# Residual rows of the attention layer: stored as centred and scaled rows, finished later by GpSimd

## The chip, the cores and the metric

One Trainium2 chip, of which the kernel uses one core. TensorE (PE in the profile, PEld for its weight loads) multiplies, VectorE (DVE), ScalarE (ACT) and GpSimd (POOL) do the elementwise work, and DMAs are issued from the queues of SyncE (SP), ACT and POOL. The metric is the device time of one execution in microseconds (us).

## What is computed

A trunk of two layers on 1024 tokens of width 1024, all in float32. Layer 0 (even) mixes with a pooling mixer and a state-space scan, layer 1 (odd) with two kinds of attention, eight heads each. Each mixer and each SwiGLU is followed by a residual sum and a layer norm.

```python
def layer_norm(x, g, b):
    mu = jnp.mean(xf, axis=-1, keepdims=True)
    var = jnp.mean(jnp.square(xf - mu), axis=-1, keepdims=True)
    return ((xf - mu) * lax.rsqrt(var + LN_EPS) * g + b).astype(x.dtype)
...
    for l in range(DEPTH):
        i = l // 2
        if l % 2 == 0:
            h = even_mixer(x, ...)
        else:
            h = odd_mixer(x, ...)
        x = layer_norm(DEEPNORM_ALPHA * x + h, ln_mix_g[l], ln_mix_b[l])
        x = layer_norm(DEEPNORM_ALPHA * x + swiglu(x, ffn_w_gate[l], ffn_w_up[l], ffn_w_down[l]),
                       ln_ffn_g[l], ln_ffn_b[l])
```

The change touches the last norm of layer 0: its output x goes into layer 1 twice, transposed as the operand of the input projection, and by rows as the residual `DEEPNORM_ALPHA * x` of the odd layer.

## The kernel before

The program is written as Python generators in the order in which they are pulled; a scheduling layer then turns that order into one instruction stream for each engine, reorders a little where operands are not ready, and hands out the buffers. Nearly all tiles in SBUF come from one pool of 50 slots of 128x1024 floats (`self.slot`); a slot is given again when all who read it are done, and an instruction that writes a new tile waits for them.

A product in float32 is made of three products of split operands: a high part (a CAST on ACT, L196) and a low part, the rest (a subtraction, L204, on DVE or POOL). Operands are called `wh`, `wl` (weights), `xT` (tokens), `kh`, `kl`, `qs` (keys and queries).

`finish` (L391) ends each mixer and each SwiGLU. For each of the eight row tiles `accs[t]` (128 tokens, 128x1024, called `accr` in the trace of layer 0's SwiGLU) it takes mean and variance, and `center` (L382) makes `(x - mean) * r` in place on ACT (L385). After every fourth tile PE transposes the tiles by columns (L312) and ACT or DVE apply scale and shift of the norm on the transposed copy (L317, L319), since there they are one number for each partition; that gives `xT`. The rows themselves still lack scale and shift. Where `rows` is given (the two mixers), the centred rows are stored to memory as they are (L425), and the SwiGLU that follows finishes them one by one on POOL (`residual`, L623 to L627: load, multiply, add, store). Where it is not given (layer 0's SwiGLU before the odd layer), a generator `late` (L436) does it: two DVE operations on each row tile with the broadcast vectors `lnv` (L439, L440), and a store from SP (L442).

The odd layer, `odd`, interleaves two generators through `weave` (L45): `filler`, which yields pieces of dense PE work (projections, called units: `q0`, `k0`, `misc`, `V0`, `v0`, `q1`, ...; at the end `G0` to `G7`, which load the residual rows from `store`, L1504), and `chain`, the sequential part, which yields how many pieces of filler to pull at each point, or the name of a unit to wait for. Before the change `chain` begins with `late`, with three pieces after each row, then waits for `misc`, pulls 5 more, and runs `f_chain`: the forget gates, their logarithm (L782 to L793), cumulative sums (L821) and, in `pairs`, their broadcast to all partitions (`bias_row`, L1684). `misc` makes the forget gate's logits and the shared rotary key in two halves of 16 products (L1263); each half is read out of PSUM by ACT (L1267, L1268) and DVE (L1269, L1270). Then come eight pairs of heads, eight steps each: scores (L1594), a softmax (L1615 or L1619, L1617, L1625), transposes of the probabilities (L1646) and the product with the values (L1664).

Of the kernel before, what the change touches and what calls it, by code (L numbers as in the profile page):

```python
# [16 lines left out]
ALU = mybir.AluOpType  # L17
# [3 lines left out]
P = 128  # L21
# [60 lines left out]
class Trunk:  # L82
# [308 lines left out]
    def finish(self, accs, gb, evac, ln=None, store=None, nxt=None, rows=None):  # L391
# [3 lines left out]
        nc = self.nc  # L395
        if ln is None:
            gb = self.ln_vecs(*gb)
            for t in range(NT):
                acc = accs[t]
                mv, r = self.ln_stats(acc, evac(t))  # L400
# [17 lines left out]
        for t in range(NT):  # L418
            acc = accs[t]
            mv, r = self.ln_stats(acc, evac(t))  # L420
            if t in (0, 2):
                next(nxt)
            self.center(acc, mv, r)
            if rows is not None:
                nc.sync.dma_start(out=rows[t * P:(t + 1) * P, :], in_=acc)  # L425
            if t == 7:
                next(nxt)
            if t % 4 == 3:
                made = self.make_xT(accs, t // 4, xT, ln) if rows is None else self.make_x7(accs, t // 4, x7, ln)
                for k, _ in enumerate(made):  # L430
                    if t == 7 and k in (self.lead_at if rows is None else self.lead7_at):
                        next(self.lead, None)
# [2 lines left out]

        def late():  # L436
            v = self.ln_vecs(*gb)
            for t in range(NT):
                nc.vector.tensor_tensor(out=accs[t], in0=accs[t], in1=v[0], op=ALU.mult)  # L439
                nc.vector.tensor_tensor(out=accs[t], in0=accs[t], in1=v[1], op=ALU.add)  # L440
                if store is not None:
                    nc.sync.dma_start(out=store[t * P:(t + 1) * P, :], in_=accs[t])  # L442
                yield 1

        self.late = late

# [772 lines left out]
    def odd(self, accs, store, spill, nxt, rows):  # L1219
# [338 lines left out]
            next(self.lead)  # L1558
        yield
        run_all(self.lead)  # L1560
        late = self.late
        rope = self.slot(name="rope")
        for r in (0, 64):
            nc.scalar.dma_start(out=rope[r:r + 64], in_=ap["rope"])
# [155 lines left out]
            return n  # L1720

        def chain():
            for _ in late():
                yield self.late_n
            yield "misc"
            yield self.misc_wait
            yield from f_chain()
# [1 line left out]
            n = 0  # L1729
            for pr in pairs():  # L1730
                if isinstance(pr, str):
                    yield pr
                    continue
                solo.clear()
                kind = 0 if n < 3 else 1 if n < 4 else 2 if n < 7 else 3
                for i, (e, u) in enumerate(self.steps[kind]):
                    if n == 3 and i == self.tag_i:
                        self.pb_tags, self.pf_tags = self.odd_tags[1]
                    elif i == 0:
                        self.pb_tags, self.pf_tags = self.odd_tags[0 if n < 4 else 2]  # L1740
                    products, nF, vv = pr[0][e]
                    if pend and self.tr_first[kind]:
                        next(pend[0])
                    prob, scale = softmax(qk(products, u), nF)
                    pend.append(pv(prob, vv, u, pr[1], e))
                    yield due(self.pace[kind][0])
                    if len(pend) > 1:
                        if self.tr_first[kind]:
                            yield due(self.pace[kind][1])
                        for k, _ in enumerate(pend.pop(0)):  # L1750
                            if k == self.scale_at[kind]:
                                scale()
                                scale = None
                            yield due(self.pace[kind][1])
                    if scale:
                        scale()
                n += 1
                seen[0] = 2 * n
# [128 lines left out]
```

## Time and profile before

| | |
|---|---|
| median of 3 runs | 2553.81 us (2553.07 to 2563.61) |
| the profiled execution | 2555.2 us, its span 2553.4 us |
| TensorE busy | 2475.8 us (97%), granted clock 0.991 on average |
| VectorE / ScalarE / GpSimd busy | 1835.8 (72%) / 1037.1 (41%) / 719.3 us (28%) |

A busy share is an average over stages; matmuls overlap in the pipeline, so "busy" for PE means that it had a matmul in flight. The names of buffers are given without their numbers, and a line (L204) can be that of a helper used everywhere. An arrow `<-` behind an idle time names what ended it.

### The profile page before, as it was taken

The numbers are of one execution on the slowest core, as the hardware profiler recorded it, in microseconds if no ns is written. First come the engines' busy times: TensorE is split into PE (matmuls) and PEld (weight loads), VectorE is DVE, ScalarE is ACT, GpSimd is POOL, SyncE is SP. The second block draws the span as 40 slices with busy tenths as digits, with TensorE's granted clock in tenths as the row PEclk, the third lists the DMA queues.
The fourth block names the chain that finished last, engine by engine and source line by source line (L and its number), as shares of the span: only waits on it lengthen the run. The fifth ranks groups of instructions, "written<-read, shape, count | busy, mean of one in ns | idle before, by whom it ended". The sixth has DMA issues, their size and how long they took to land.

```text
span 2553.4 us, 31570 instructions
## 1 busy us (share of the span) xinstructions
PE 2475.8 (97%) x11886; PEld 2000.4 (78%) x11886; DVE 1835.8 (72%) x2922; ACT 1037.1 (41%) x1742; POOL 719.3 (28%) x422
## 2 busy tenths in 40 slices
PE   8999999999999999998999999898999999999998
PEld 6778877778888878886787777777877888887887
DVE  4354554788778769976655566687779778777998
ACT  3343344352222233453344455565544232233453
POOL 2444442103433432112011112211011434433113
PEclk9999999999999999999999999998999999999999
DMA  4111013224433447322100002012322433426641
GB/s 171 50 34 42 25 44 130 79 83 146 151 112 132 149 161 280 108 91 96 66 23 28 34 25 56 20 42 83 118 89 95 141 127 124 146 101 256 214 153 71
DMA packets 92954, 261.48 MB, mean 102 GB/s; under 512 B 9697, under 2 KB 9953, under 8 KB 92801
## 3 DMA queue, kind: packets, MB, share of 16 engines
q1 hardware_dynamic: 84480, 230.56, 26.0%
q0 software_dynamic: 5568, 18.94, 2.1%
q10 hardware_dynamic: 2752, 9.96, 1.1%
q8 instruction: 94, 1.54, 0.3%
q14 instruction: 60, 0.48, 0.1%
HBM read 185.89 MB, written 71.30 MB: 101 GB/s over the span
## 4 chain that ended last, share of the span: by engine, by line
PE 85%; DVE 7%; issue 3%; ACT 3%; POOL 1%; DMA 1%; SPq 0%; DVEq 0%; ACTq 0%; POOLq 0%
PE p L497 7%; PE p L498 7%; PE p L499 7%; PE pa L237 5%; PE pa L239 4%; PE pa L238 4%; PE pa L1594 4%; PE pa L499 3%; PE pa L497 3%; PE p L237 3%; PE pa L498 3%; PE p L239 3%; PE p L238 3%; PE p L633 3%; PE p L635 3%; PE p L634 3%
## 5 line engine op out<-in xcount | busy, mean ns | idle before, releaser
L204 DVE TENSOR_TENSOR w<-wr,w 128x512 fp32r<-128x512 f32 x440 | 415.9, 968 | 105.0 <-ACT w L196 99.2
L196 ACT CAST w<-wr 128x512 fp32r<-128x512 f32 x440 | 251.6, 619 | 428.7 <-DVE wr L480 331.8
L497 PE MATMUL p<-x,w 128*128 128x512 f32 x848 | 331.3, 392 | 6.4 <-ACT w L196 4.8
L498 PE MATMUL p<-x,w 128*128 128x512 f32 x848 | 331.2, 391 | 0.5 <-DVE x L204 0.4
L499 PE MATMUL p<-x,w 128*128 128x512 f32 x848 | 330.8, 390 | 0.1
L545 POOL TENSOR_TENSOR h<-h,c 128x1024 f32<-128x1024 f32 x44 | 114.4, 2601 | 572.0 <-DVE c L538 419.8
L204 POOL TENSOR_TENSOR wl<-wr,wh 128x1024 fp32r<-128x1024 f32 (+2 forms) x55 | 133.0, 2421 | 447.0 <-ACT wh L196 415.8
L497 PEld LDWEIGHTS p<-x,w 128*128 128x128 f32 x848 | 159.2, 188 | 43.4 <-ACT w L196 6.4
L498 PEld LDWEIGHTS p<-x,w 128*128 128x128 f32 x848 | 159.3, 188 | 35.7 <-DVE x L204 3.5
L499 PEld LDWEIGHTS p<-x,w 128*128 128x128 f32 x848 | 159.2, 188 | 33.8 <-DVE w L204 1.0
L237 PE MATMUL pa<-xh,wh 128*128 128x512 f32 x368 | 149.1, 405 | 1.9 <-ACT u L900 1.1
L497 PE MATMUL pa<-x,w 128*128 128x512 f32 x384 | 149.5, 389 | 0.0
L498 PE MATMUL pa<-x,w 128*128 128x512 f32 x384 | 149.5, 389 | 0.0
L499 PE MATMUL pa<-x,w 128*128 128x512 f32 x384 | 149.5, 389 | 0.0
L239 PE MATMUL pa<-xh,wl 128*128 128x512 f32 x368 | 144.6, 393 | 4.4 <-POOL wl L204 4.4
L238 PE MATMUL pa<-xl,wh 128*128 128x512 f32 x368 | 144.4, 392 | 0.0
L633 PE MATMUL p<-w,h 128*128 128x512 f32 x352 | 138.4, 394 | 3.6 <-DVE c L540 3.6
L634 PE MATMUL p<-w,h 128*128 128x512 f32 x352 | 138.2, 393 | 0.0
L635 PE MATMUL p<-w,h 128*128 128x512 f32 x352 | 138.0, 393 | 0.0
L204 DVE TENSOR_TENSOR h<-hr,h 128x512 fp32r<-128x512 f32 x154 | 123.5, 802 | 10.7 <-ACT h L196 10.6
L196 ACT CAST h<-hr 128x512 fp32r<-128x512 f32 x154 | 95.2, 618 | 73.6 <-DMA hr<-parts 36.4
L635 PE MATMUL pa<-w,h 128*128 128x512 f32 x264 | 102.9, 390 | 0.0
(405 smaller groups left out, 5960.8 us busy)
## 6 DMA issues: line engine op xcount, KB each, us to landing
hr<-parts SPq DMA_DIRECT2D x70, 512.0 KB, 4.3
wr<-in_ffn_w_gate_dram SPq DMA_DIRECT2D x44, 512.0 KB, 4.0
wr<-in_ffn_w_up_dram SPq DMA_DIRECT2D x44, 512.0 KB, 4.1
wr<-in_ffn_w_down_dram SPq DMA_DIRECT2D x44, 512.0 KB, 8.9
parts<-s SPq DMA_DIRECT2D x80, 256.0 KB, 2.1
accr<-rows SPq DMA_DIRECT2D x32, 512.0 KB, 3.7
parts<-h SPq DMA_DIRECT2D x60, 256.0 KB, 2.1
wr<-in_even_wt_dram SPq DMA_DIRECT2D x24, 512.0 KB, 3.7
```

Of the source, the lines that this page charges most:

```text
L196: self.nc.scalar.copy(out=out, in_=in_)
L204: eng.tensor_tensor(out=out, in0=in_, in1=hi.bitcast(F32), op=ALU.subtract)
L237: mm(out=out, lhsT=lh, rhs=rh, start=i == 0, stop=False)
L238: mm(out=out, lhsT=lh, rhs=rl, start=False, stop=False)
L239: mm(out=out, lhsT=ll, rhs=rh, start=False, stop=i == n - 1)
L497: mm(out=out, lhsT=ah, rhs=b[k][:, lo], start=k == 0, stop=False)
L498: mm(out=out, lhsT=ah, rhs=b[k][:, hi], start=False, stop=False)
L499: mm(out=out, lhsT=al, rhs=b[k][:, lo], start=False, stop=k == 3)
L545: pt(out=h, in0=h, in1=c, op=ALU.mult)
L633: mm(out=out, lhsT=ah, rhs=b[:, lo], start=first, stop=False)
L634: mm(out=out, lhsT=ah, rhs=b[:, hi], start=False, stop=False)
L635: mm(out=out, lhsT=al, rhs=b[:, lo], start=False, stop=last)
```

## The change

The centred rows are now stored by `finish` in this case too, from SP, right after `center`. `late` no longer works on the tiles in SBUF: its first pull loads the two vectors, and each further pull loads one row tile from `store` (SP), multiplies and adds on GpSimd, and stores it back from GpSimd's queue. `chain` no longer begins with it; it is pulled in every second step of the attention pairs from the second pair on: the vectors at step 1 of the second pair, rows 0 to 2 in that pair, rows 3 to 6 in the third, row 7 in the fourth.

```diff
@@ finish
             self.center(acc, mv, r)
-            if rows is not None:
-                nc.sync.dma_start(out=rows[t * P:(t + 1) * P, :], in_=acc)
+            out = store if rows is None else rows
+            if out is not None:
+                nc.sync.dma_start(out=out[t * P:(t + 1) * P, :], in_=acc)
...
         def late():
             v = self.ln_vecs(*gb)
+            yield
             for t in range(NT):
-                nc.vector.tensor_tensor(out=accs[t], in0=accs[t], in1=v[0], op=ALU.mult)
-                nc.vector.tensor_tensor(out=accs[t], in0=accs[t], in1=v[1], op=ALU.add)
-                if store is not None:
-                    nc.sync.dma_start(out=store[t * P:(t + 1) * P, :], in_=accs[t])
-                yield 1
+                r = self.load_raw(store[t * P:(t + 1) * P, :], name="res")
+                nc.gpsimd.tensor_tensor(out=r, in0=r, in1=v[0], op=ALU.mult)
+                nc.gpsimd.tensor_tensor(out=r, in0=r, in1=v[1], op=ALU.add)
+                nc.gpsimd.dma_start(out=store[t * P:(t + 1) * P, :], in_=r)
+                yield
@@ odd
-        late = self.late
+        late = self.late()
@@ odd, chain
-            for _ in late():
-                yield self.late_n
             yield "misc"
...
                         next(pend[0])
+                    if n and i % 2:
+                        next(late, None)
                     prob, scale = softmax(qk(products, u), nF)
```

Lines behind the change stand two lower in the new file (L1269 becomes L1271).

On DVE, at the start of the odd layer, between the key unit's last operations (`kl`, `kh`) and the read-out of the first half of `misc` (`kr`), before:

```order
L204 TENSOR_TENSOR kl_8898<-p_1400_9019,kh_8897 64x512
L1333 COPY kh_8896<-kh_8896 64x512
L1333 COPY kh_8897<-kh_8897 64x512
L439 TENSOR_TENSOR accr_7376<-accr_7376,lnv_8963 128x1024
L439 TENSOR_TENSOR accr_7438<-accr_7438,lnv_8963 128x1024
L440 TENSOR_TENSOR accr_7376<-accr_7376,lnv_8965 128x1024
L440 TENSOR_TENSOR accr_7438<-accr_7438,lnv_8965 128x1024
L1269 TENSOR_TENSOR kr_9053<-kr_9053,pa_9055 8x512
L1270 TENSOR_TENSOR kr_9053<-t_9054,pa_9055 32x512
```

The same place on DVE now:

```order
L1335 COPY kh_8904<-kh_8904 64x512
L204 TENSOR_TENSOR kl_8906<-p_1398_9017,kh_8904 64x512
L204 TENSOR_TENSOR kl_8906<-p_1398_9017,kh_8905 64x512
L1335 COPY kh_8905<-kh_8905 64x512
L1271 TENSOR_TENSOR kr_9048<-kr_9048,pa_9050 8x512
L1272 TENSOR_TENSOR kr_9048<-t_9049,pa_9050 32x512
```

The sixteen operations on `accr` are gone from DVE, and the read-out follows the key unit at once. On PE the second half of `misc` now stands 23 products of `V0`/`v0` behind the first, where it stood 58 behind it, and `f_chain` with its broadcasts (L1684) stands wholly among the products of `v0`, where it reached into the unit `q1`.

On GpSimd, in the second and third pair of heads, where `wl` is the low part of a unit's weights and `sq` a sum of squares, before:

```order
L204 TENSOR_TENSOR wl_10354<-wr_9759,wh_10353 128x1024
L204 TENSOR_TENSOR wl_10501<-wr_10162,wh_10500 128x1024
L1396 TENSOR_TENSOR sq_10169<-sq_10169,sq_10358 128x1024
L204 TENSOR_TENSOR wl_10675<-wr_10351,wh_10674 128x1024
L204 TENSOR_TENSOR wl_10840<-wr_10498,wh_10839 128x1024
```

And now:

```order
L204 TENSOR_TENSOR wl_10350<-wr_9751,wh_10349 128x1024
L442 TENSOR_TENSOR resr_10412<-resr_10412,lnv_10234 128x1024
L443 TENSOR_TENSOR resr_10412<-resr_10412,lnv_10236 128x1024
L444 DMA store<-resr_10412 128x1024
L1398 TENSOR_TENSOR sq_10159<-sq_10159,sq_10354 128x1024
L204 TENSOR_TENSOR wl_10530<-wr_10152,wh_10529 128x1024
L442 TENSOR_TENSOR resr_10592<-resr_10592,lnv_10234 128x1024
```

Between two weight splits there now stands, eight times, a pair of operations on a residual row and the issue of its store.

On SP's queue, at the end of layer 0's SwiGLU, where `hr` are the last loads of that SwiGLU and `wmr`, `wr` the first weights of the odd layer, before:

```order
L580 DMA hr_8485<-parts 128x512
L225 DMA wmr_8970<-in_odd_wm_dram 128x320
L225 DMA wr_8977<-in_odd_wv_dram 128x1024
L225 DMA wr_8979<-in_odd_wv_dram 128x1024
L442 DMA store<-accr_7160 128x1024
L225 DMA wr_8981<-in_odd_wt_dram 128x1024
```

And now:

```order
L426 DMA store<-accr_7376 128x1024
L582 DMA hr_8447<-parts 128x2x512
L582 DMA hr_8468<-parts 128x2x512
L582 DMA hr_8489<-parts 128x512
L426 DMA store<-accr_7438 128x1024
L426 DMA store<-accr_7512 128x1024
L426 DMA store<-accr_7572 128x1024
L426 DMA store<-accr_7632 128x1024
L225 DMA wmr_8971<-in_odd_wm_dram 128x320
L225 DMA wr_8978<-in_odd_wv_dram 128x1024
```

Four stores now stand ahead of the last three `hr` loads, and four ahead of the odd layer's first weights.

## Rows read from the trace of the kernel before

**Rows 1.** The page: busy time by engine, and the chain that ended last

```profile
PE 2475.8 (97%) x11886; PEld 2000.4 (78%) x11886; DVE 1835.8 (72%) x2922; ACT 1037.1 (41%) x1742; POOL 719.3 (28%) x422
...
PE 85%; DVE 7%; issue 3%; ACT 3%; POOL 1%; DMA 1%; SPq 0%; DVEq 0%; ACTq 0%; POOLq 0%
```

**Rows 2.** Waits of PE, 1180 to 1260 us: total, times, longest

```profile
PE pa L1263 <- DVE kr L1270: 3.9, 1, 3.9
PE p L238 <- POOL wl L204: 2.6, 1, 2.6
PE p L1293 <- DVE sp L793: 1.2, 1, 1.2
...
PE pa L1263 <- DVE wm L204: 0.7, 1, 0.7
...
PE p L821 <- DVE dup L814: 0.4, 1, 0.4
```

**Rows 3.** Windows: busy us of PE, PEld, DVE, ACT, POOL, clock, DMA share, GB/s

```profile
1200.00:1220.00 20.00, 13.46 (x80) 11.79 (x80) 19.74 (x16) 3.52 (x5) 8.23 (x3) 0.91 0.50 190
...
1300.00:1400.00 100.00, 99.66 (x556) 79.18 (x555) 49.80 (x105) 43.98 (x89) 12.03 (x5) 1.00 0.08 27
1400.00:1440.00 40.00, 37.84 (x174) 27.87 (x173) 21.45 (x44) 16.58 (x35) 7.39 (x3) 0.96 0.12 41
...
1580.00:1740.00 160.00, 149.28 (x875) 121.90 (x875) 121.80 (x224) 99.80 (x210) 29.17 (x15) 0.98 0.12 39
```

**Rows 4.** Timeline of PE: the two halves of misc (start, duration, idle before)

```profile
1196.53 3.91 PE L1263 MATMUL pa<-xT,wm 128*128 128x512 f32 x16 [0.67 <-DVE wm L204]
...
1214.17 5.52 PE L1263 MATMUL pa<-xT,wm 128*128 128x512 f32 x16 [3.91 <-DVE kr L1270]
```

**Rows 5.** Timeline of DVE, 1193 to 1214 us

```profile
1193.35 1.23 DVE L439 TENSOR_TENSOR accr<-accr,lnv 128x1024 f32<-128x1024 f32 x1 [1.11 <-DMA lnv<-in_ln_ffn_g_dram]
...
1205.97 4.47 DVE L439 TENSOR_TENSOR accr<-accr,lnv 128x1024 f32<-128x1024 f32 x2
1210.37 2.35 DVE L440 TENSOR_TENSOR accr<-accr,lnv 128x1024 f32<-128x1024 f32 x2
1212.74 0.68 DVE L1269 TENSOR_TENSOR kr<-kr,pa 8x512 f32<-8x512 f32 x1
```

**Rows 6.** Timeline of POOL, 1196 to 1201 us: the split of V0's weights

```profile
1198.22 4.91 POOL L204 TENSOR_TENSOR wl<-wr,wh 128x1024 fp32r<-128x1024 f32 x1 [8.85 <-ACT wh L196]
```

**Rows 7.** Lines 625 and 627: POOL's residual rows in the SwiGLUs (ns min/median/max)

```profile
L625 POOL TENSOR_TENSOR accr<-accr,lnv x16: 2382/2393/2395, 606.9 to 2255.6; 128x1024 f32<-128x1024 f32 x16
...
L627 POOL DMA_DIRECT2D rows<-accr x16: 577/586/593, 614.5 to 2263.2; - x16
```

**Rows 8.** Waits of PE, 1260 to 1580 us: total, times, longest

```profile
PE p L1646 <- DVE pt L204: 4.3, 3, 2.2
...
PE p L1405 <- DVE diag L204: 0.9, 1, 0.9
```

**Rows 9.** POOL's groups of elementwise work, 1260 to 1580 us: busy, mean ns

```profile
L204 POOL TENSOR_TENSOR wl<-wr,wh 128x1024 fp32r<-128x1024 f32 (+2 forms) x15 | 34.8, 2321 | 220.8 <-ACT wh L196 202.3 <-issue 18.4
L1396 POOL TENSOR_TENSOR sq<-sq,sq 128x1024 f32<-128x1024 f32 x4 | 10.0, 2493 | 30.3 <-ACT sq L1389 30.3
```

**Rows 10.** Timelines of DVE and POOL, 1400 to 1414 us

```profile
1402.67 0.42 DVE L1333 CAST kh<-kh 64x512 fp32r<-64x512 f32 x1
...
1410.30 2.26 DVE L1333 CAST kh<-kh 64x512 fp32r<-64x512 f32 x1
...
1409.91 2.37 POOL L204 TENSOR_TENSOR wl<-wr,wh 128x1024 fp32r<-128x1024 f32 x1 [16.48 <-ACT wh L196]
```

**Rows 11.** Timelines of SP and ACT around the turn to the odd layer

```profile
1163.56 0.35 SPq L225 DMA_DIRECT2D wmr<-in_odd_wm_dram  x1
...
1169.57 1.24 ACT L385 ACTIVATE accr<-accr,nmr,rs 128x1024 f32<-128x1024 f32 x1 [1.19 <-DVE nmr L384]
...
1190.37 0.71 ACT L196 CAST wm<-wmr 128x256 fp32r<-128x256 f32 x2
```

## The prediction, written before the changed kernel ran

> **What bounds the kernel now.** I read the page first, then the windows, the waits of TensorE and the timelines around the two places that the change touches. TensorE has a matmul in flight for 97% of the span and carries 85% of the chain that ended last [rows 1]. So VectorE's 72% matter only where TensorE waits for VectorE. The change takes work from VectorE at the turn to the odd layer (1190 to 1225 us) and gives work to GpSimd in the attention that follows (some 1360 to 1570 us). Both places have to be priced in TensorE's waits.
>
> At the turn TensorE stands still: in the window from 1200 to 1220 us it is busy for 13.46 of 20 us, while VectorE is busy for 19.74 [rows 3]. The list of waits names why [rows 2]: 3.9 us before the second half of `misc`, until VectorE had read out the first half (L1270); 2.6 us for the low part of `V0`'s weights from GpSimd; 0.7 us for VectorE's `wm`; 1.2 and 0.4 us for two steps of the forget gate's chain. Together 8.8 us. In the attention TensorE hardly waits: 99.66 of 100 us are busy from 1300 to 1400 us [rows 3].
>
> **What is removed.** Sixteen operations of 1.2 us on VectorE, eight stores from SP behind them, and an early load of the two vectors. They matter through what queues behind them on VectorE:
> - The first half of `misc` ends on TensorE at about 1200.4 us (1196.53 and 3.91) [rows 4]. Its read-out L1269 begins on VectorE only at 1212.74, because two pairs of `accr` operations of 4.47 and 2.35 us stand directly ahead [rows 5]. Without them it comes some 7 us earlier (12.74 less 5.97, the start of that block, is 6.8), and TensorE meanwhile has 23 products of `V0` in front of the second half. The 3.9 us wait goes.
> - The wait of 0.7 us for `wm` goes: the operation ahead of it on VectorE is the first `accr` one, which itself waited for the vectors' load [rows 5].
> - GpSimd's split of `V0`'s weights took 4.91 us [rows 6], where such splits and sums elsewhere take 2.3 to 2.5 [rows 9]; VectorE ran `accr` operations meanwhile. At 2.4 us it ends at 1200.6. TensorE got there at 1200.6 (its wait of 2.6 ended when the split did, at 1203.1), now 0.7 us earlier, at 1199.9. About 0.7 us of the wait stays; bounds 0 and 2.6.
> - The 1.2 and 0.4 us in the forget gate's chain I leave as they are: the chain moves to a place with about as much TensorE work in front of it, and the rotary key's five operations move in between its links. Bounds: both gone, or 3 us more, if two or three of these, as long as an `accr` operation (2.35 us for two, [rows 5]), come in between.
>
> So 8.8 less 0.7, 1.2 and 0.4 gives 6.5 us. To that comes the clock. After the stall the same 16 products took 5.52 us instead of 3.91 [rows 4], and the granted clock over the window is 0.91 [rows 3], a part of it at 1.2 instead of 2.4 GHz: 0.09 of 20 us is 1.8 us, close to 5.52 less 3.91. The longest wait left there is about 1 us, and stretches with so little idle time have the full clock (1.00 from 1300 to 1400 us), so I count the 1.8 us as given back. **Gain at the turn: 8.3 us**; bounds 4 (the chain of the forget gate 3 us worse, half of the clock lost) and 10.6 (all waits gone).
>
> **What is added.** In `finish`, eight stores on SP. The first four stand ahead of the last three `hr` loads, but their rows are centred well before those loads could go (they wait for slots that are freed by the transposes after it), so nothing moves. The other four stand ahead of the odd layer's first weights. The last waits for the centring that ends at 1170.8 us, so `wmr` is issued there and not at 1163.6; ACT casts it at 1190.37 [rows 11]. 20 us remain for a load: nothing. If that cover were gone, the cost would be these 7 us. From then on SP has no `accr` store to wait for, and the tiles' slots come free earlier.
>
> In the attention, on GpSimd: per row a product and a sum of 2.39 us each (the sum at L626 is an operation of the same kind and size) and 0.59 us for the store's issue [rows 7], as in the SwiGLUs. Eight rows: 38.2 us of elementwise work and 4.7 us of issue (8 times 0.59). GpSimd has room: it is busy for 12 of 100 us [rows 3]. What is queued behind them are the weight splits (L204). One of them stands in front of nearly each pair; before, GpSimd sat idle 221 us in front of 15 splits [rows 9], so a split that is late by 5.4 us, or by the landing of a row's load on top, still comes long before its unit. The loads on SP stand in a row of weight loads that are issued two units ahead. Both: nothing. Readers of the finished rows (`G0` to `G7`) come after the attention's last pairs, far later than row 7.
>
> The price is on VectorE. Its copy of a half key, L1333, takes 0.42 us, and 2.26 us when GpSimd is at work: it starts at 1410.30, GpSimd's split ends at 1412.28, the copy at 1412.56 [rows 10]. Behind it stood `pt`, and TensorE waited for it 2.2 us, the longest wait of the attention's first half [rows 8]. The window around it has a clock of 0.96, that is 1.6 us more in 40 [rows 3].
>
> The Trainium skill says the same in "SBUF — State Buffer", section "Who interferes with whom": GpSimd shares its port pair with VectorE as an exclusive lock for a whole instruction, and whoever comes second blocks fully; VectorE's copies, scalings and operations with two inputs from SBUF are hit. The trace agrees (0.42 to 2.26 us). By that rule a row could hold VectorE for up to 4.8 us; the rows decide how often that reaches TensorE.
>
> How often it does I take as a rate. From 1260 to 1580 us GpSimd did 19 splits and sums, 44.8 us [rows 9]; TensorE waited for VectorE's `pt` and `diag` 5.2 us in all [rows 8]. Put wholly down to GpSimd that is 0.116 us per us. For 38.2 us: 4.4 us, and in the same proportion 1.4 us of clock. **Cost in the attention: 5.8 us.** Bounds: 0 (most splits hit nothing: 15 of 19 are followed by no wait of TensorE, since four waits make up the 5.2 us), and eight times the worst one, 2.2 us and 1.6 us of clock, 30 us.
>
> **Sum.** 5.8 less 8.3 is 2.5 us less. The profiled execution took 2555.2 us (span 2553.4 and 1.8 around it): 2552.7. It is 1.4 us above the median of the runs, 2553.8; there the sum gives **2551.3 us**. No change can be told from 0.5% here, 12.8 us.
>
> **The rivals.**
> - *GpSimd's work is hidden.* The scheduler puts the rows where VectorE has operations that read PSUM, and those do not slow down beside GpSimd. For it: most splits cost nothing. Against it: the pairs are twice as long as a split, and the wait at 1411 us is a plain case. Then the turn's gain stands alone: 2553.8 less 8.3, 2545.5 us.
> - *The lock decides* (the other side). Each row meets one of VectorE's copies or scalings in front of a tile that TensorE waits for, and costs as much as the one at 1410 us: 8 times 3.8 is 30 us, less 8.3: 2576 us. It is slower from 8.3 us on, that is from 1 us per row on, and measurably so (2566.6) from 2.6 us per row. Against it: TensorE has filler, and one in nineteen did this.
> - *The slots decide.* The two vectors and one or two rows take three or four of 50 slots during three pairs of heads, and the first operation on a row waits on GpSimd for a load that waits for a slot; the splits queue behind it. If one unit comes late by a pair and a split, 4.8 and 2.4 us, it is 7.2 us above the forecast: 2558.5 us. For it: SP's loads do wait for slots in the attention. Against it: the eight `accr` tiles no longer hold slots at the turn, and the loads are far ahead.
> - *The attention falls into better step.* `f_chain` no longer reaches into `q1`, the first scores come earlier, and the filler kept back serves later pairs, which wait. TensorE is idle for 10.7 of the 160 us from 1580 on [rows 3]; if a third of that went and the turn gave its upper bound without cost in the attention, it would be 2553.8 less 10.6 and 3.6, 2539.6 us. Against it: those waits are in pairs of the other kind, which the change doesn't reach.
>
> **How the numbers follow.** The forecast (gain 6 to 9, cost 3 to 9 us) 0.50; hidden 0.24; slots 0.10; lock 0.10; better step 0.06. The time given is that of the likeliest. The range from 2543 to 2564 us leaves out most of the lock and of the better step, and holds both bounds of the turn (2553.8 less 10.6 is 2543.2) and a cost of three times the rate (17.4 less 8.3 is 9.1: 2562.9). The forecast's own range is 2548 to 2557. Faster by over 0.5% (below 2541): 0.06 and a little of the hidden case, 0.08. Slower by over 0.5%: most of the lock, a little of the slots, 0.10. Within 0.5%: 0.82.
>
> **What would show it.** Right, if the wait of L1263 for `kr` and the clock's 0.91 are gone from the turn, the split of `V0` takes some 2.4 us, and in the second to fourth pair GpSimd's rows stand beside some L1333 or L1625 of 2 us and more, with 8 to 12 us of waits in TensorE where there were 6. Wrong, if TensorE at the turn waits for something that the `accr` operations only hid (the forget gate's chain above all), if GpSimd's operations on a row take far more than 2.4 us, or if TensorE's waits after 1580 us differ by more than 5 us; those I took as unchanged.

## The result, and the profile after

The changed kernel is slower: a median of 2570.4 us (2564.5 to 2579.3, ten runs) beside 2555.6 us (2553.1 to 2563.6, ten runs) for the kernel before, a ratio of 1.0052 with a 95% interval from 1.0039 to 1.0065. Forecast were 2551.3 us, with a range from 2543 to 2564, and that a change under 0.5% could not be told; the interval here is 0.13% to either side. The profiled execution took 2573.6 us, with a span of 2571.4 us and a mean granted clock of 0.985 (0.991 before). Work has moved from VectorE to GpSimd as written [rows 1]; this is the page after:

```profile
PE 2489.5 (97%) x11886; PEld 2008.6 (78%) x11886; DVE 1820.9 (71%) x2906; ACT 1035.8 (40%) x1742; POOL 758.7 (30%) x446
```

The turn came out much as forecast. The waits of PE from 1180 to 1260 us (total, times, longest), to be read beside [rows 2], have lost the 3.9 us for `kr`, the 0.7 for `wm` and the 0.4 for `dup`:

```profile
PE p L238 <- POOL wl L204: 1.1, 1, 1.1
PE p L237 <- DVE kl L204: 1.1, 1, 1.1
...
PE p L1295 <- DVE sp L795: 0.2, 1, 0.2
```

The two halves of `misc` in PE's timeline now both run at the full rate (3.91 and 5.52 us in [rows 4]):

```profile
1197.37 3.79 PE L1265 MATMUL pa<-xT,wm 128*128 128x512 f32 x16
1205.06 3.82 PE L1265 MATMUL pa<-xT,wm 128*128 128x512 f32 x16
```

And GpSimd's split of `V0`'s weights takes 2.38 us where it took 4.91 [rows 6]:

```profile
1199.90 2.38 POOL L204 TENSOR_TENSOR wl<-wr,wh 128x1024 fp32r<-128x1024 f32 x1 [11.50 <-ACT wh L196]
```

The loss is in the attention. Two windows show it, the turn and the 320 us behind it, columns as in [rows 3]. Before:

```profile
1180.00:1260.00 80.00, 68.70 (x388) 55.29 (x386) 59.21 (x90) 27.81 (x48) 17.60 (x10) 0.98 0.31 107
1260.00:1580.00 320.00, 313.19 (x1643) 241.60 (x1641) 191.01 (x382) 156.52 (x307) 55.40 (x36) 0.99 0.12 34
```

After:

```profile
1180.00:1260.00 80.00, 76.10 (x431) 62.00 (x430) 41.77 (x89) 32.09 (x57) 13.67 (x8) 0.98 0.09 26
1260.00:1580.00 320.00, 303.77 (x1488) 231.44 (x1487) 180.26 (x339) 139.58 (x271) 93.64 (x56) 0.93 0.19 60
```

Read each row twice. The length less TensorE's busy time is its idle time; the length times (1 less the clock) is an estimate of what the clock took. At the turn idle time fell from 11.3 to 3.9 us and the clock stayed the same. In the attention idle time rose from 6.8 to 16.2 us, and the clock's part from 3.2 to 22.4 us (the clock has two digits, so 1.6 us either way). That is 28.6 us lost against 7.4 won, 21.2 in all; the spans differ by 18.0. From 1580 to 1920 us the changed kernel lost some 6 us less than the kernel before, nearly all of it to the clock, so the tally closes only to within the rounding of the clocks. These are windows of one execution each; the means over all runs, in the table below, show a smaller part for the clock.

The waits of PE from 1333 to 1580 us in the changed kernel, beside [rows 8]:

```profile
PE p L1648 <- DVE pt L204: 4.8, 5, 1.4
PE p L1666 <- ACT diag L196: 3.5, 2, 3.3
PE p L1407 <- POOL sq L1398: 2.4, 1, 2.4
PE p L1666 <- DVE diag L204: 1.7, 1, 1.7
PE p L1648 <- DVE prob L1627: 1.5, 1, 1.5
```

The waits that are followed here end with an engine that was itself held up. The longest, 3.3 us for `diag`, goes back to a slot. ACT's timeline shows a cast that stood ahead of `diag`:

```profile
1392.28 1.04 ACT L196 CAST wh<-wr 128x1024 fp32r<-128x1024 f32 x1 [5.29 <-DMA store<-resr]
1393.23 0.47 ACT L196 CAST diag<-p 128x384 fp32r<-128x384 f32 x1
```

`wh` is a new tile and reads no row, yet it waited for a row's store to land: it was given the slot that the row had just left. POOL's timeline has the row: GpSimd waited 3.71 us for its load, and issued its store at 1389.26.

```profile
1384.06 2.38 POOL L442 TENSOR_TENSOR resr<-resr,lnv 128x1024 f32<-128x1024 f32 x1 [3.71 <-DMA resr<-store]
1386.51 2.45 POOL L443 TENSOR_TENSOR resr<-resr,lnv 128x1024 f32<-128x1024 f32 x1
1389.26 0.60 POOL L444 DMA_DIRECT2D store<-resr  x1 [0.30 <-PE p L1648]
...
1495.48 2.54 POOL L442 TENSOR_TENSOR resr<-resr,lnv 128x1024 f32<-128x1024 f32 x1 [28.13 <-DMA resr<-store]
1498.10 3.22 POOL L443 TENSOR_TENSOR resr<-resr,lnv 128x1024 f32<-128x1024 f32 x1
```

The last two of these rows hold VectorE. Its timeline beside them:

```profile
1495.82 3.29 DVE L206 SCALAR_TENSOR_TENSOR latl<-craw,vec,lath 128x1024 fp32r<-128x1024 f32 x1
1499.03 2.90 DVE L1627 TENSOR_SCALAR prob<-prob,l 128x384 f32<-128x384 f32 x2
1501.86 0.68 DVE L204 TENSOR_TENSOR pt<-p,pt 128x512 fp32r<-128x512 f32 x1
```

`latl` takes 1.28 us where no GpSimd operation runs beside it (e3 below); here 3.29. `pt`, which TensorE waits for, stands behind both.

### The profile page after: what moved, and what is told of

It reads as the page before. It is cut to its first block, busy times and chain, and to the rows that moved or that the text cites. A ratio compares the mean times of both kernels' runs of the same rounds, so it can differ in the third digit from the quotient of the medians.

```text
span 2571.4 us, 31617 instructions
## 1 busy us (share of the span) xinstructions
PE 2489.5 (97%) x11886; PEld 2008.6 (78%) x11886; DVE 1820.9 (71%) x2906; ACT 1035.8 (40%) x1742; POOL 758.7 (30%) x446
## 4 chain that ended last, share of the span: by engine, by line
PE 84%; DVE 7%; issue 4%; ACT 3%; POOL 2%; DMA 1%; SPq 0%; DVEq 0%; ACTq 0%; POOLq 0%
PE p L499 7%; PE p L501 7%; PE p L500 7%; PE pa L237 5%; PE pa L239 4%; PE pa L238 4%; PE pa L1596 4%; PE pa L501 3%; PE pa L499 3%; PE p L237 3%; PE pa L500 3%; PE p L238 3%; PE p L239 3%; PE p L636 3%; PE p L637 3%
```

## The experiments

Theories at the start: **slots** (the rows' loads, stores and slots hold up in-order queues), **lock** (GpSimd's operations hold VectorE), **step** or **order** (the attention's earlier start is itself the trouble). All kernels of a group ran on one chip with the kernel before. The last four columns: "at full clock" is the mean over the runs of span times granted clock, a measure that leaves the clock out, and "to the clock" is the rest of the span (for the kernel before 2528 to 2529, and 26 to 30, by the groups that have its clocks); then idle time and clock loss in the window from 1260 to 1580 us of the one profiled execution, read as above.

| kernel | median us (before) | ratio, 95% interval | at full clock | to the clock | idle | clock |
|---|---|---|---|---|---|---|
| before | 2555.6 | | 2528 | 26 to 30 | 6.8 | 3.2 |
| changed | 2570.4 (2555.6) | 1.0052, 1.0039 to 1.0065 | 2533.8 | 34.9 | 16.2 | 22.4 |
| e1 no rows | 2560.2 (2558.4) | 1.0002, 0.9987 to 1.0017 | 2525.0 | 33.3 | 9.0 | 12.8 |
| e2 thin operations | 2559.4 (2558.4) | 1.0001, 0.9986 to 1.0016 | 2528.7 | 28.1 | 10.7 | 12.8 |
| e3 no loads and stores | 2576.7 (2558.4) | 1.0060, 1.0039 to 1.0081 | 2531.7 | 40.1 | 15.5 | 22.4 |
| e4 rows in `G` units | 2574.8 (2558.4) | 1.0064, 1.0044 to 1.0083 | 2533.7 | 39.0 | 9.0 | 12.8 |
| e6 e1, sums on VectorE | 2555.7 (2554.5) | 0.9993, 0.9977 to 1.0009 | 2520.7 | 30.2 | 7.3 | 3.2 |
| e7 rows on VectorE | 2557.6 (2554.5) | 1.0008, 0.9996 to 1.0019 | 2530.2 | 25.6 | 12.8 | 6.4 |
| e8 quarters | 2568.4 (2554.5) | 1.0059, 1.0037 to 1.0080 | 2535.2 | 33.0 | 18.7 | 12.8 |
| e9 quarters, sums | 2564.3 (2554.5) | 1.0029, 1.0015 to 1.0044 | 2532.4 | 29.9 | 14.9 | 9.6 |
| e11 one slot | 2576.7 (2558.5) | 1.0065, 1.0040 to 1.0091 | 2537.2 | 36.9 | 20.0 | 16.0 |
| e13 one slot, sums | 2571.1 (2558.5) | 1.0051, 1.0034 to 1.0068 | 2535.5 | 34.3 | 22.7 | 12.8 |
| e14 before, sums | 2561.8 (2558.5) | 1.0018, 1.0001 to 1.0036 | 2529.9 | 31.0 | 9.0 | 3.2 |
| e15 paced, one slot | 2574.8 (2557.5) | 1.0070, 1.0043 to 1.0098 | 2537.2 | 36.0 | 19.6 | 12.8 |
| e12 rows, sums on VectorE | 2559.5 (2557.5) | 1.0001, 0.9986 to 1.0017 | 2528.3 | 29.0 | 12.7 | 9.6 |
| e16 e15, splits on VectorE | 2562.7 (2562.5) | 1.0010, 0.9995 to 1.0025 | 2525.8 | 35.0 | 9.4 | 12.8 |
| e17 e1, splits on VectorE | 2542.3 (2562.5) | 0.9922, 0.9901 to 0.9943 | 2515.4 | 22.9 | 0.7 | 3.2 |
| e18 changed, splits on VectorE | 2557.8 (2562.5) | 0.9994, 0.9979 to 1.0010 | 2528.7 | 27.9 | 9.0 | 6.4 |
| e19 all on VectorE | 2552.9 (2559.1) | 0.9976, 0.9957 to 0.9995 | 2524.7 | 26.8 | 6.9 | 6.4 |
| e20 before, splits on VectorE | 2546.9 (2556.3) | 0.9957, 0.9939 to 0.9974 | 2521.5 | 24.1 | 3.9 | 3.2 |

**e1, no rows.**

```diff
-                    if n and i % 2:
-                        next(late, None)
```

> Leaves out scale and shift of the residual rows: the centred rows are stored, and nothing finishes them later (no vectors, no loads, no elementwise work, no stores in the attention). What is left of the change is the turn and an attention that begins earlier. If the rows' own work cost the time (theory 'slots': their loads, stores and slots hold up in-order queues; or theory 'lock': GpSimd's operations hold up VectorE), the turn's gain stands alone: 8 to 11 us below the kernel before, about 2545 to 2548, and the spill stores of the later pairs come some 10 us earlier than before. If the attention's earlier start is itself the trouble (theory 'step': the filler and the chain now meet in a worse place, and the rows are innocent), it is near the changed kernel, about 2565 to 2572.

Between the two theories, and so both have a share: without any row the turn's gain is gone all the same. In the window the attention has lost 2.2 us more to waits and 9.6 more to the clock than before; over all runs on this chip e1 is 3.7 us better than the kernel before at full clock and gives 4.5 back to the clock. The waits of PE from 1333 to 1580 us name a newcomer, and POOL's timeline its reason:

```profile
PE p L1407 <- POOL sq L1398: 4.2, 2, 2.8
```

```profile
1446.77 2.40 POOL L204 TENSOR_TENSOR wl<-wr,wh 128x1024 fp32r<-128x1024 f32 x1 [13.39 <-ACT wh L196]
1449.13 2.65 POOL L1398 TENSOR_TENSOR sq<-sq,sq 128x1024 f32<-128x1024 f32 x1
```

A weight split now stands on GpSimd ahead of a sum of squares that TensorE needs next. In the kernel before this sum ran ahead of the split (at 1452.08, the split at 1456.85), and TensorE did not wait for it.

**e2, thin operations** (16 of 1024 columns), **and e3, no loads and stores:**

```diff
-                nc.gpsimd.tensor_tensor(out=r, in0=r, in1=v[0], op=ALU.mult)
+                nc.gpsimd.tensor_tensor(out=r[:, 0:16], in0=r[:, 0:16], in1=v[0][:, 0:16], op=ALU.mult)
...  (the sum likewise)
```

```diff
-                r = self.load_raw(store[t * P:(t + 1) * P, :], name="res")
-                nc.gpsimd.tensor_tensor(out=r, in0=r, in1=v[0], op=ALU.mult)
+                r = self.slot(name="resr")
+                nc.gpsimd.tensor_tensor(out=r, in0=v[1], in1=v[0], op=ALU.mult)
                 nc.gpsimd.tensor_tensor(out=r, in0=r, in1=v[1], op=ALU.add)
-                nc.gpsimd.dma_start(out=store[t * P:(t + 1) * P, :], in_=r)
```

> Leaves out scale and shift of 1008 of the 1024 columns: loads, slots, vectors, waits and stores of the rows stay as in the changed kernel, but GpSimd's two operations on a row work on 16 columns. Theory 'slots': still near the changed kernel, 2562 to 2572, with ACT's cast of a weight waiting for a row's store and GpSimd waiting some us for a row's load. Theory 'lock': the cost goes with the elementwise work, 2545 to 2549. Half and half would be about 2557.

> Leaves out the finished rows: a row's two operations on GpSimd keep their size and place, but the first takes the two vectors as its inputs, and there is no load and no store of a row; its slot is free again when the second operation ends. The elementwise work and the two vectors' slots stay. Theory 'slots': most of the cost goes, 2547 to 2554. Theory 'lock': near the changed kernel, 2565 to 2572, with VectorE's copies and scalings of 2 us and more in the second to fourth pair and TensorE waiting behind them.

Theory "slots", as it stood, falls. With all loads, slots and stores but hardly any GpSimd work the rows cost nothing beside e1; with the work and no transfer they cost all of it. GpSimd's elementwise time is the price. Not only the lock shows in e3, though. Here a new tile of VectorE waits for a row's operation whose result it does not read; both timelines:

```profile
1493.51 1.28 DVE L206 SCALAR_TENSOR_TENSOR latl<-craw,vec,lath 128x1024 fp32r<-128x1024 f32 x1 [2.57 <-POOL resr L443]
```

```profile
1491.09 2.39 POOL L443 TENSOR_TENSOR resr<-resr,lnv 128x1024 f32<-128x1024 f32 x1
```

**e4, the rows finished in the units `G0` to `G7`:**

```diff
                 nc.sync.dma_start(out=a, in_=store[t * P:(t + 1) * P, :])
+                if t == 0:
+                    lv.extend(self.lnv())
+                nc.gpsimd.tensor_tensor(out=a, in0=a, in1=lv[0], op=ALU.mult)
+                nc.gpsimd.tensor_tensor(out=a, in0=a, in1=lv[1], op=ALU.add)
```

> The whole computation: each of the units G0 to G7, which loads a residual row anyway, has it multiplied and added to by GpSimd in that same tile before VectorE adds the product; no store and no second load. The two vectors are loaded with G0. Theory 'slots': no extra slot, load or store for the rows apart from the two vectors, so the turn's gain stays, 2545 to 2550. Theory 'lock': sixteen operations now stand where VectorE is busy for 84 of 100 us, so it should cost there as much as it did in the attention, 2560 to 2575.

As dear as in the attention, though no row is left there (its window reads as e1's). The waits of PE from 1740 to 1920 us have a new first line, where the sum on VectorE stands behind the row's operations:

```profile
PE p L237 <- DVE acc L1520: 9.1, 4, 4.6
```

So this is a dependency beside whatever the lock does, and no proof of the lock.

**e6, e1 with the sums of squares on VectorE; e14, the control on the kernel before:**

```diff
-                        nc.gpsimd.tensor_tensor(out=lst["ss"], in0=lst["ss"], in1=sq, op=ALU.add)
+                        nc.vector.tensor_tensor(out=lst["ss"], in0=lst["ss"], in1=sq, op=ALU.add)
```

> As e1 (centred rows stored, nothing finishes them: scale and shift of the residual rows are left out), and the sums of squares L1398 run on VectorE, not on GpSimd. In e1 TensorE waited 4.2 us in the third pair for these sums, because GpSimd took a weight split of 2.4 us ahead of each of two of them; in the kernel before they stood ahead of the splits. Theory 'order': that flip is what ate the turn's gain, with the clock behind it; the wait goes, and the time falls from 2560 to 2546 to 2551. Rival 'any gap will do': the attention is so tight that the next late operand takes the place of this one; 2556 to 2561.

> The whole computation, a control: the kernel before with nothing but its sums of squares moved to VectorE. TensorE waits for no sum there, so nothing is to be won: no change, 0.998 to 1.002 of before. If it is faster by as much as e6 is than e1 (0.003), then the move helps by itself, and theory 'order' is not shown by e6.

In e6 the profiled execution kept the gain (window: 7.3 idle, 3.2 clock; 2545.4 us), but its runs lie between 2544.8 and 2560.5, and its interval overlaps that of e1. TensorE still waits 2.0 us, now for VectorE's sum. The control won nothing; it was slower, if anything (1.0018). "Order" is supported, not shown.

**e7, the rows on VectorE, and e12, the sums too:**

```diff
-                nc.gpsimd.tensor_tensor(out=r, in0=r, in1=v[0], op=ALU.mult)
+                nc.vector.tensor_tensor(out=r, in0=r, in1=v[0], op=ALU.mult)
...  (the sum likewise; e12: the edit of e6 as well)
```

> The whole computation: as the changed kernel, but a row's two operations run on VectorE and not on GpSimd (loads, slots and stores as they are). Theory 'lock': no GpSimd operation of 2.4 us holds VectorE; VectorE itself has 16 operations of 1.2 us more, so a tile is late by 1.2 and not by 2.4 us or more, and about half of the 16 us goes: 2562 to 2567. Rival 'late sums': what costs is GpSimd's own queue (splits and sums of squares behind a row), so nearly all goes: 2557 to 2560. Rival 'VectorE's time': its own 19 us cost as much as GpSimd's 38: 2569 to 2576.

> The whole computation: the rows' operations on VectorE as in e7, and the sums of squares on VectorE too. TensorE does not wait for a sum in e7, so by theory 'order' nothing is to be won: 2554 to 2560. If it is 2550 or less, it is the version that beats both kernels.

The same 16 operations cost 11 us less (0.0044 of 2556, by the two ratios) on the engine that TensorE waits for most than on the one that seemed idle: 19.6 us of VectorE (16 of 1.22) in place of 40.0 of GpSimd. That is the range of "late sums", but the move takes away both the hold on VectorE and the queue on GpSimd, so it does not tell these apart. The sums add nothing, as expected.

**e8, a row's operations in quarters, and e9, the sums on VectorE too:**

```diff
+                for c in range(0, 1024, 256):
+                    s = slice(c, c + 256)
+                    nc.gpsimd.tensor_tensor(out=r[:, s], in0=r[:, s], in1=v[0][:, s], op=ALU.mult)
+                    nc.gpsimd.tensor_tensor(out=r[:, s], in0=r[:, s], in1=v[1][:, s], op=ALU.add)
```

> The whole computation: as the changed kernel, but each of a row's two operations on GpSimd is cut into four of 256 columns (the same work in shorter pieces). Theory 'lock': VectorE is held for one short piece, about 0.6 us, and not for 2.4 us, so most of the 16 us goes: 2558 to 2564. Rival 'queue': what counts is how long GpSimd is occupied with a row, which is the same or longer: 2569 to 2576.

> The whole computation: as e8, with the sums of squares on VectorE as in e6. Theories 'lock' and 'order' together: the turn's gain is left over, 2547 to 2553, the first version that beats the kernel before. If only 'order' holds: 2560 to 2566. If neither: 2570.

Shorter pieces do not help. The test is not clean: a quarter takes 0.80 and 0.76 us on the mean, so a row occupies GpSimd for 6.2 us and not 5.0, and the wait for `diag` behind a row's slot grows to 5.1 us. e9 is some 4 us better than e8 by the medians; it is slower than the kernel before, and not clearly faster than the changed one (the intervals touch).

**e11, one slot kept for all rows, and e13, the sums on VectorE too:**

```diff
             v = self.ln_vecs(*gb)
+            r = self.slot(name="resr")
...
-                r = self.load_raw(store[t * P:(t + 1) * P, :], name="res")
+                nc.sync.dma_start(out=r, in_=store[t * P:(t + 1) * P, :])
```

> The whole computation: as the changed kernel, but all eight rows go through one slot that is taken once and kept until the last store. Loads, GpSimd's operations and stores are the same in number and size (and, since a row no longer waits for a free slot, they come closer together, in the second and the first half of the third pair). No other tile is given a slot that a row has just left. Theory 'slots': what costs is that ACT's and VectorE's new tiles are given a row's slot and wait in their queues for GpSimd's operation or for the store's landing; those waits go, and the time falls to that of the kernel without elementwise work, 2555 to 2561. Theory 'lock': GpSimd's 38 us hold VectorE as before; 2566 to 2574.

> The whole computation: as e11, with the sums of squares on VectorE as in e6. If 'slots' and 'order' are the two causes, both are gone: 2549 to 2555. If only 'order' helps: 2562 to 2568. If the sums were not in the way here: as e11.

No gain, and the largest single wait, 7.3 us, does not come from the lock. It is again a slot, but not a row's own: ACT's `pt` waits for a weight split, the last reader of its slot, and the split stands on GpSimd behind a row that waited for its load. In e13 the same kind of wait costs TensorE 10.0 us, with the sums gone from GpSimd. POOL's timeline and ACT's in e11:

```profile
1383.60 2.33 POOL L443 TENSOR_TENSOR resr<-resr,lnv 128x1024 f32<-128x1024 f32 x1 [5.87 <-DMA resr<-store]
1385.89 2.33 POOL L204 TENSOR_TENSOR wl<-wr,wh 128x1024 fp32r<-128x1024 f32 x1
```

```profile
1388.26 0.58 ACT L196 CAST pt<-p 128x512 fp32r<-128x512 f32 x1 [7.32 <-POOL wl L204]
```

**e15, operations of the rows' size in one kept slot, paced by each step, without transfers:**

```diff
+            r = self.slot(name="resr")
...
-                r = self.load_raw(store[t * P:(t + 1) * P, :], name="res")
-                nc.gpsimd.tensor_tensor(out=r, in0=r, in1=v[0], op=ALU.mult)
+                nc.gpsimd.tensor_tensor(out=r, in0=v[0], in1=self.nm_.to_broadcast([P, 1024]), op=ALU.mult)
...
-                nc.gpsimd.dma_start(out=store[t * P:(t + 1) * P, :], in_=r)
```

> Leaves out the finished rows (no load and no store of a row): GpSimd does sixteen operations of the size of the rows' at the rows' places, but in one slot that is kept, and each first operation reads a statistic of the step before, so that it stands at its step and waits for no load. No tile is given a slot that such an operation holds; what is left of the rows is GpSimd's time itself, for VectorE's port and for the weight splits and sums of squares queued behind. The kernel without any rows took 2558 (e1), the one with the same operations in slots that are given back 2575 (e3). If tiles that wait for a row's slot are the cost: 2556 to 2562. If GpSimd's time is: 2570 to 2577. In between, the two share it, and the traces say in what parts.

GpSimd's time it is, though the first operation, with a statistic as its second input, is somewhat shorter (1.90 us). The longest wait of TensorE there, 4.19 us at 1372.63, in POOL's timeline and ACT's: a row's two operations, a sum behind them, and ACT's `pt` waiting for the slot that the sum frees.

```profile
1364.87 1.90 POOL L442 TENSOR_TENSOR resr<-lnv,nm 128x1024 f32<-128x1024 f32 x1 [16.10 <-DVE nm L1616]
1366.84 2.50 POOL L443 TENSOR_TENSOR resr<-resr,lnv 128x1024 f32<-128x1024 f32 x1
1369.31 2.65 POOL L1397 TENSOR_TENSOR sq<-sq,sq 128x1024 f32<-128x1024 f32 x1
```

```profile
1371.99 0.59 ACT L196 CAST pt<-p 128x512 fp32r<-128x512 f32 x1 [5.58 <-POOL sq L1397]
```

**e16, e17 and e18, the attention's weight splits and sums on VectorE,** on top of e15, of e1 and of the changed kernel, so that nothing stands behind a row on GpSimd:

```diff
         for c in self.order:
             units.append(pool[c].pop(0))
+            self.att.add(units[-1][0])
...
-            spl.append(self.split(raw[n], cols=units[n][2], eng=self.nc.vector if units[n][0][0] in self.dve or
+            spl.append(self.split(raw[n], cols=units[n][2], eng=self.nc.vector if units[n][0] in self.att or units[n][0][0] in self.dve or
...  (and the edit of e6)
```

> Leaves out the finished rows, as e15 (sixteen paced operations on GpSimd in one kept slot). The attention's weight splits and sums of squares run on VectorE, so that in the second to fourth pair GpSimd has nothing but the rows' operations, and nothing can stand behind them; VectorE's port is shared as before. To be compared with e17, the same without the rows' operations. Theory 'queue' (what costs is what stands behind a row on GpSimd, and the slots it frees late): at most 4 us over e17. Theory 'port' (VectorE is held): 10 us or more over e17.

> Leaves out scale and shift of the residual rows, as e1. The attention's weight splits and sums of squares run on VectorE; GpSimd does no elementwise work in the second to fourth pair. Control for e16. Some 15 us more of VectorE's time, no wait for a sum of GpSimd and no VectorE copy held: 2548 to 2560.

> The whole computation: the changed kernel, rows on GpSimd with their loads, slots and stores, and the attention's weight splits and sums of squares on VectorE. Theory 'queue': most of the cost goes, 2555 to 2561; what is left are tiles that wait for a row's own slot. Theory 'port': 2566 or more.

e16 stands 20 us above e17 (by the medians), with no split or sum queued behind the rows on GpSimd: VectorE is held. Its timeline in e16, and POOL's beside it:

```profile
1437.69 2.59 DVE L1398 TENSOR_TENSOR sq<-sq,sq 128x1024 f32<-128x1024 f32 x1
1440.20 3.38 DVE L205 TENSOR_TENSOR wl<-wr,wh 128x1024 fp32r<-128x1024 f32 x1
1443.50 0.68 DVE L205 TENSOR_TENSOR pt<-p,pt 128x512 fp32r<-128x512 f32 x1
```

```profile
1437.30 1.90 POOL L443 TENSOR_TENSOR resr<-lnv,nm 128x1024 f32<-128x1024 f32 x1 [12.63 <-DVE nm L1618]
1439.28 3.22 POOL L444 TENSOR_TENSOR resr<-resr,lnv 128x1024 f32<-128x1024 f32 x1
```

`sq` ends 1.08 us after the first GpSimd operation, `wl` 1.08 us after the second: each waited for it and then took about its own time, 1.21 and 1.22 us on the mean in e17. The second GpSimd operation, begun while `sq` was still at work, in its turn took 3.22 and not 2.39 us [rows 7]. TensorE waited 3.17 us for the `pt` behind them. The Trainium skill, "SBUF — State Buffer", section "Who interferes with whom", states this: a VectorE operation with two inputs in SBUF and a GpSimd operation that reads SBUF block each other fully, whichever comes second. These rows agree.

A held VectorE also frees slots late. The next longest wait of TensorE in e16, 2.72 us at 1369.19, is for ACT's `pt`, and that waited 4.10 us for a slot whose last reader was a `sq` of 3.40 us on VectorE.

In e17 TensorE waits for hardly anything; all its waits from 1333 to 1580 us, and the window:

```profile
PE p L1668 <- ACT pt L197: 0.4, 2, 0.2
PE p L1650 <- DVE prob L1629: 0.2, 1, 0.2
```

```profile
1260.00:1580.00 320.00, 319.33 (x1679) 246.94 (x1678) 205.70 (x409) 162.66 (x316) 19.00 (x22) 0.99 0.12 35
```

e18, the whole computation, lies in the range of "queue" (2555 to 2561). That does not speak for it, since the range left out what the move of splits and sums is worth by itself, 0.0080 by the ratios of e1 and e17, 20 us. Against e17, which shares that move, the rows still cost 0.0072, 18 us; against e1, with splits and sums on GpSimd, they cost 0.0050, 13 us in the changed kernel. So the rows' price did not go with the queue behind them. Both ways, a held VectorE and a late slot, are open to a GpSimd operation, as the rows above show.

**e19, e18 with the rows on VectorE, and e20, the kernel before with splits and sums on VectorE:**

> The whole computation: as e18, but the rows' two operations run on VectorE too, so that GpSimd does no elementwise work in the second and third pair, and only issues the rows' stores. If GpSimd's elementwise time is what costs (held VectorE, late slots), the version without rows (e17, 2542) is nearly reached: rows on VectorE cost nothing measurable in e7 against e1, so 2542 to 2550, faster than the kernel before by 0.3 to 0.6%. If VectorE's own time is now the limit (some 15 us of splits and sums and 19 us of rows more in 240 us): 2553 to 2562, no better than e7.

> The whole computation: the kernel before, its rows finished on VectorE at the turn as they were, with nothing but the attention's weight splits and sums of squares moved from GpSimd to VectorE. If GpSimd's elementwise time costs TensorE in the attention whatever the rows do (held VectorE, late slots), it keeps e17's attention and pays the turn's 7 to 9 us: 2546 to 2551, faster than before by 0.2 to 0.5%. If the attention of the kernel before is free of it (TensorE idles for 6.8 of 320 us there, at a clock of 0.99), there is little to win: 2552 to 2560.

Both beat the kernel before, e19 by 0.2% and e20 by 0.4%, and the changed one with it; e20 is the best whole version. e19 missed its first range (2542 to 2550) and ends at the rim of the second: it stands 0.0054, 14 us, above e17, where rows on VectorE had cost nothing measurable in e7 against e1. With splits and sums there too, VectorE's own time counts.

The gain of e20 came in another place than expected: most at the turn (5.8 us idle, before 11.3), 2.9 us in the attention. At the turn GpSimd now does two weight splits in place of three; the two copies L1333 ahead of `kr` take 1.49 us (3.58 before), and TensorE's wait for `kr` is 0.7 us (3.9 before), with the `accr` operations still in their place. Windows of e20:

```profile
1180.00:1260.00 80.00, 74.18 (x413) 59.80 (x412) 61.07 (x102) 29.61 (x52) 11.74 (x8) 0.98 0.31 107
1260.00:1580.00 320.00, 316.10 (x1658) 243.62 (x1656) 202.06 (x402) 159.86 (x312) 18.11 (x21) 0.99 0.11 34
```

## Why the prediction was wrong, step by step

- **The gain at the turn: right for the waits.** Forecast were 6.5 us of waits and 1.8 of the clock; 7.4 and 0 came. The split of `V0` took 2.38 us (2.4 said), the waits for `kr` and `wm` are gone, and those in the forget gate's chain fell from 1.6 to 0.2 us. The clock over 1180 to 1260 us is 0.98 in both kernels. The 0.91 from 1200 to 1220 us did go (1.00 now), but a stretch that had 1.00 before fell, behind three waits of 0.6 to 1.1 us:

```profile
1190.00:1200.00 10.00, 9.76 (x36) 7.96 (x37) 4.64 (x11) 3.33 (x6) 0.10 (x1) 0.83 0.00 0
```

- **"The price is on VectorE ... How often it does I take as a rate": one of two steps that failed.** 4.4 us of waits and 1.4 of the clock stood there, 5.8 in all. By the ratios (1.0052 less 1.0002 for e1, of 2556) the rows cost 12.8 us, some 5 to either side. The rate was drawn from the waits for `pt` and `diag` alone, at a time when GpSimd was busy for 17% of the window (55.4 of 320 us); it is 29% now, and the second way, slots, did not enter it. How the price divides is less sure: the profiled executions show 7.2 us more of idle time and 9.6 more to the clock in the window (changed kernel less e1), the means over all runs 8.8 at full clock and 1.6 to the clock.
- **"Both: nothing", of the splits queued behind a row and the loads: wrong for the splits.** Asked was whether a split comes late for its unit. It comes in time for that; but it is the last reader of a slot that ACT or VectorE gets for a tile needed at once (7.3 us in e11; the sums likewise, 5.6 us in e15). For loads and stores by themselves it held (e2).
- **The attention taken as unchanged by an earlier start: the other step that failed.** It was no term of the sum at all, put at nothing without a reason; only a gain from it was a rival. Without any row the turn's forecast 8.3 us should stand alone, but e1 is level with the kernel before (1.0002, so 0.5 us slower): 8.8 us are missing. With the 7.0 us by which the rows were priced too low that makes 15.8, all that lies between 2.5 us less and the 13.3 us more that the ratio gives. By e1's trace the cause is the split ahead of the sum; e6 makes that likely and does not show it, and e17 shows that the loss goes when neither is on GpSimd.
- **The rivals.** "GpSimd's work is hidden" falls with e2 and e3. "The lock decides" was nearest in time (2576) and has its mechanism shown in e16 and in the rows at 1495 us; but the price per row is 1.6 us (12.8 / 8), not 3.8, late slots have a share in it, and the 8.3 us that it took off for the turn were not there. So two errors of opposite sign brought it near. "The slots decide" named the right waits (a row's first operation on its load, 3.7 and 28.1 us) with the wrong sufferer. "Better step" had the sign wrong. Most signs named for a right forecast came (no wait for `kr`, a split of 2.38 us, VectorE operations of 2 us and more beside rows); the one that did not was the size of TensorE's waits, 16.2 us and not 8 to 12.

**Open:** how the rows' price divides between a held VectorE and late slots. Followed one by one in the changed kernel, a row's slot made TensorE wait 3.3 us (`diag`), a VectorE operation held beside a row 0.7 and 1.4 us (`pt`, at 1410.6 and 1502.6), one held beside a split or a sum 1.2 and 1.5 us (`pt` at 1448.8, `prob` at 1520.9), and a sum behind a split 2.4 us, as in e1. So part of what the rows cost comes from where splits and sums meet VectorE once the rows have moved them. No run removes one of these and leaves the others in place.

## What to carry to other kernels

An idle engine is not a free one. Before work goes to GpSimd, list what VectorE does with two SBUF operands or as a copy in that stage, and which tiles GpSimd is the last to read, since a new tile can be given a slot whose last reader is late, and then the queue of its writer stops (2.7 to 10.0 us of TensorE's time here). Do not price the clock as a small share of the new gaps: over all runs the changed kernel lost some 5 us more at full clock and 5 to 9 more to the clock than the kernel before. And where a stall is removed ahead of a tightly woven stage, look at what the stage does when it starts earlier, with an experiment that does only that.

## What the chip showed that was not expected

The clock can fall well after a gap, and while TensorE is busy. In the changed kernel TensorE was idle for 4.7 us from 1380 to 1400 us, with a granted clock of 0.66 in the second half; it ran at 1.00 and 0.99 while it was busy for 9.89 and 9.37 of the next two stretches of ten, and then, busy throughout, ran for ten us wholly at the lower level, 1.2 GHz: 22 matmuls. Windows:

```profile
1380.00:1390.00 10.00, 8.59 (x45) 5.92 (x44) 8.30 (x16) 5.48 (x12) 5.78 (x4) 1.00 0.34 105
1390.00:1400.00 10.00, 6.73 (x24) 5.36 (x23) 3.56 (x8) 4.55 (x8) 2.37 (x1) 0.66 0.13 52
1400.00:1410.00 10.00, 9.89 (x55) 7.97 (x53) 8.37 (x17) 4.50 (x11) 2.68 (x2) 1.00 0.19 54
1410.00:1420.00 10.00, 9.37 (x45) 7.03 (x46) 7.31 (x12) 3.93 (x8) 6.49 (x4) 0.99 0.49 158
1420.00:1430.00 10.00, 10.00 (x22) 5.52 (x22) 1.52 (x5) 3.40 (x9) 4.01 (x3) 0.50 0.13 52
```

Nor is a gap always there: in e17 TensorE had a matmul in flight for all of 1280 to 1540 us, and from 1440 to 1450 us its clock was 0.83. What brings the clock down in such a place no run here shows.

```profile
1440.00:1450.00 10.00, 10.00 (x48) 7.79 (x47) 6.45 (x17) 5.64 (x10) 0.00 (x0) 0.83 0.00 0
```

Runs of one kernel differ mainly in this: e17's six have clocks from 0.989 to 0.994 and times from 2534 to 2544 us. The span times its clock varies less, and tells kernels apart that the times alone do not (e1 and e6: 2525.0 and 2520.7 us, with overlapping intervals of their ratios).
